# A two-layer decoder trunk: three quarters of each MLP's first matrix by Strassen's method, laced with the second matrix

## The chip, the cores and the metric

The kernel runs on one core of a Trainium2 chip. The metric is the device time of one execution in microseconds (us); lower is better. TensorE multiplies, VectorE and ScalarE work between the products, GpSimd helps outside the MLPs, SyncE (SP) issues the DMAs.

## The reference

Two layers act on a residual stream h of 528 tokens (16 meta tokens and 512 others) by 1024 features. Each layer adds a token mixer (a retention and convolution mixer in the first layer, stick-breaking attention in the second) and then an MLP. The output is h without the meta tokens, so the second layer's MLP needs only 512 tokens. What the change touches is the MLP, with w1 of 1024 x 4096 and w2 of 4096 x 1024:

```python
def sq_relu_mlp(h, w1, w2):
    return jnp.square(jax.nn.relu(h @ w1.astype(h.dtype))) @ w2.astype(h.dtype)
h = h + sq_relu_mlp(rmsnorm(h, norm_mlp_g[layer]), mlp_w1[layer], mlp_w2[layer])
```

## The kernel before

Everything is held transposed: h is eight tiles of 128 features by 528 tokens (`h[m]`), so a product has weights as the stationary operand (128 x 128) and tokens as the moving columns. Each float32 operand is used as a high and a low part, and each product is three matmuls (`products`, L280): high x high, high x low, low x high.

**Weight blocks.** A unit is a block of weights for one 128-row piece of an output: 1024 x 128 values, a 512 KB tile of 128 x 1024. `unit_order` (L94) writes down all 218 in the order of use: 40 of the first mixer's w_in, 16 of w_out, 64 of the first MLP, 24 of attention (queries, keys and values for each p of 0 to 7), 10 of its output, 64 of the second MLP. `load` (L163) has SP fetch the next block into one of two `raw` tiles. `prepare` (L176) takes it apart: ScalarE copies it to the high tile `whi` (L195), VectorE subtracts that to get `wlo` (L196); both have three buffers. `gemm` (L286) calls `weights`, which hands out the oldest prepared unit and prepares the one two places behind it; then `gemm` runs 8 x 3 products into a PSUM tile `mm` of two banks. There are two such tiles. A block is 48 matmuls over 264 columns where all 528 tokens are needed (two halves, each in a bank), and 24 matmuls over 512 columns in the second layer's MLP.

**The MLP** (`mlp`, L793) goes through `MLP_STEPS` (L116): four chunks of w1 of eight blocks each, and w2's four chunks between and behind them. After the first block `rstd` works out the normalisation factor `rb` of every token. Each w1 block's result is evicted by one VectorE operation (L808: maximum with 0, times `rb`), squared twice on ScalarE (L810, high part, and L811) and brought to a low part by VectorE (L812). Each w2 block is added to `h[m]` by VectorE (L387).

**What sets the order.** Outside the MLPs the kernel is written inside `tc.manual_schedule(engines=...)`: TensorE, VectorE, ScalarE and GpSimd then issue in the order in which the program emits their instructions, while SP's order stays the scheduler's. In the MLPs of the kernel before the scheduler orders all engines. In attention, queries, keys and values of p each start with `weights`, and so emit the load of the unit two ahead; the K copies of p (L968) are emitted by the chain that `keys` leaves behind, in the first step of the queries of p + 1, behind that unit's load.

## Time and profile before

| | us |
|---|---|
| median of 3 runs (1399.53 to 1400.27) | 1400.21 |
| the profiled execution | 1400.1 |
| its span in the profile | 1398.3 |
| TensorE busy in the span | 1377.2 |
| VectorE busy | 878.2 |
| ScalarE busy | 606.3 |
| GpSimd busy | 358.0 |

The span begins and ends with the profile's first and last instruction; the execution's own time has 1.8 us around it. The granted clock of TensorE is 0.998 of full speed over the span. Busy time of a matmul is modelled from its own start to the end of its passage, so neighbours overlap: what a matmul costs in a dense stretch is the distance between starts.

### The profile page before, as it was taken

The page shows a single profiled execution, that of the slowest core. Times are in us where ns is not written, and L with a number is a line of the kernel's source. Part 1 is how long each engine was busy: PE and PEld are TensorE (multiplying, and loading weights), DVE is VectorE, ACT ScalarE, POOL GpSimd, SP SyncE. Part 2 cuts the span into 40 slices and gives each one's busy share as a digit, 9 for nine tenths or more (in the row PEclk, how much of TensorE's full clock was granted, in tenths as well). Part 3 has the DMA queues.
Part 4 walks back from the last instruction along what each step waited for, and adds up shares of the span by engine and source line. Part 5 has one row for each costly group of instructions (what it writes and reads, how often), then busy time and mean ns, then how long its engine had stood idle before and what let it go on. Part 6 is the DMA issues. An engine that isn't in the chain of part 4 may idle for free.

```text
span 1398.3 us, 23379 instructions
## 1 busy us (share of the span) xinstructions
PE 1377.2 (98%) x9396; PEld 1270.3 (91%) x9396; DVE 878.2 (63%) x1461; ACT 606.3 (43%) x1136; POOL 358.0 (26%) x414
## 2 busy tenths in 40 slices
PE   8999999999999999999999999998999999999998
PEld 7999999999999999999999888997877888888887
DVE  5998999966344434334345899999985443434332
ACT  5434545567443313223132677776554422313220
POOL 2656455356500000000016433335640000000000
PEclk9999999999999999999999999999999999999999
DMA  5322221122322222222322534333323223232332
GB/s 189 106 91 86 66 71 67 62 76 93 100 96 92 91 91 92 91 91 91 91 91 88 141 107 122 107 107 91 91 91 101 95 93 103 91 106 91 98 105 83
DMA packets 39643, 134.00 MB, mean 96 GB/s; under 512 B 4976, under 2 KB 5104, under 8 KB 39536
## 3 DMA queue, kind: packets, MB, share of 16 engines
q1 hardware_dynamic: 39536, 132.52, 30.3%
q8 instruction: 74, 1.21, 0.4%
q14 instruction: 33, 0.27, 0.1%
HBM read 117.69 MB, written 2.10 MB: 86 GB/s over the span
## 4 chain that ended last, share of the span: by engine, by line
PE 91%; DVE 6%; issue 1%; ACT 1%; POOL 0%; DMA 0%; POOLq 0%; SPq 0%; ACTq 0%; DVEq 0%
PE mm L284 72%; PE qk L284 10%; PE pz L1034 1%; PE po L1066 1%; DVE E L1043 1%; PE pw L1056 1%; PE po L696 1%; DVE mT L1077 1%; PE po L700 1%; PE po L698 0%; DVE acc L492 0%; DVE hdn L595 0%; DMA h<-xT 0%; PE pv L682 0%; PE pt L754 0%
## 5 line engine op out<-in xcount | busy, mean ns | idle before, releaser
L195 ACT CAST whi<-raw 128x256 fp32r<-128x256 f32 (+1 forms) x338 | 212.2, 659 | 490.3 <-PE mm L284 455.2
L196 POOL TENSOR_TENSOR wlo<-raw,whi 128x256 fp32r<-128x256 f32 (+1 forms) x334 | 280.6, 859 | 284.1 <-ACT whi L195 134.6
L196 DVE TENSOR_TENSOR wlo<-raw,whi 128x1024 fp32r<-128x1024 f32 (+1 forms) x134 | 165.3, 1234 | 23.0 <-ACT whi L195 15.8
L387 DVE TENSOR_TENSOR h<-mm,h 128x528 f32<-128x528 f32 (+1 forms) x64 | 44.9, 701 | 207.7 <-PE mm L284 207.7
L492 DVE SCALAR_TENSOR_TENSOR acc<-cx,ptm,acc 128x526 f32<-128x526 f32 (+28 forms) x232 | 157.6, 740 | 3.5 <-ACT cx L487 3.5
L284 PE MATMUL mm<-xnh,whi 128*128 128x264 f32 x640 | 135.6, 294 | 0.0
L284 PE MATMUL mm<-xnl,whi 128*128 128x264 f32 x640 | 130.8, 285 | 3.1 <-DVE xnl L320 2.7
L284 PE MATMUL mm<-xnh,wlo 128*128 128x264 f32 x640 | 129.9, 285 | 0.0
L284 PE MATMUL mm<-x1h,whi 128*128 128x264 f32 x512 | 104.1, 285 | 0.0
L284 PEld LDWEIGHTS mm<-xnl,whi 128*128 128x128 f32 x640 | 100.1, 190 | 4.1 <-DVE xnl L320 3.0
L284 PEld LDWEIGHTS mm<-xnh,whi 128*128 128x128 f32 x640 | 100.9, 190 | 2.9 <-issue 1.3
L284 PE MATMUL mm<-x1l,whi 128*128 128x264 f32 x512 | 103.2, 283 | 0.0
L284 PE MATMUL mm<-x1h,wlo 128*128 128x264 f32 x512 | 102.8, 282 | 0.0
L284 PE MATMUL mm<-x3l,whi 128*128 128x512 f32 x256 | 99.7, 390 | 0.5 <-DVE x3l L320 0.5
L284 PE MATMUL mm<-x3h,whi 128*128 128x512 f32 x256 | 100.0, 391 | 0.0
L284 PE MATMUL mm<-x3h,wlo 128*128 128x512 f32 x256 | 99.6, 389 | 0.0
L284 PEld LDWEIGHTS mm<-xnh,wlo 128*128 128x128 f32 x640 | 99.6, 190 | 0.0
L334 POOL TENSOR_TENSOR n2s<-n2q,n2q 128x528 f32<-128x528 f32 x1 | 1.9, 1865 | 334.7 <-ACT n2q L353 334.7
L284 PE MATMUL qk<-x2h,whi 128*128 128x264 f32 (+1 forms) x320 | 82.9, 323 | 0.5 <-ACT kraw L926 0.5
L808 DVE SCALAR_TENSOR_TENSOR r<-mm,m0rb 128x528 f32<-128x528 f32 x32 | 22.6, 707 | 93.7 <-PE mm L284 93.7
L284 PEld LDWEIGHTS mm<-x1l,whi 128*128 128x128 f32 x512 | 79.5, 188 | 0.0
L284 PEld LDWEIGHTS mm<-x1h,whi 128*128 128x128 f32 x512 | 79.0, 188 | 0.1
(400 smaller groups left out, 3333.3 us busy)
## 6 DMA issues: line engine op xcount, KB each, us to landing
raw<-wts SPq DMA_DIRECT2D x217, 512.0 KB, 3.5
Q<-qhl SPq DMA_DIRECT2D x32, 256.0 KB, 4.5
K<-khl SPq DMA_DIRECT2D x32, 132.0 KB, 3.6
h<-xT SPq DMA_DIRECT2D x8, 264.0 KB, 6.1
out<-h SPq DMA_DIRECT2D x8, 256.0 KB, 2.0
ctm<-con SPq DMA_DIRECT2D x1, 790.0 KB, 6.9
raw<-wts SPq DMA_DIRECT2D x2, 256.0 KB, 4.0
ca<-con SPq DMA_DIRECT2D x1, 256.0 KB, 6.0
```

What stands on the lines that cost most here:

```text
L195: copy(hi[:, ks], raw[:, ks])
L196: eng.tensor_tensor(lo[:, ks], raw[:, ks], hi[:, ks].bitcast(F32), ALU.subtract)
L284: nc.tensor.matmul(p, a[:, k, :], b[:, sl], start=(first and t == 0), stop=(last and t == 2))
L387: nc.vector.tensor_tensor(v2(h[m][:, :n], n), ps, v2(h[m][:, :n], n), ALU.add)
L492: nc.vector.scalar_tensor_tensor(a, cxf[:, s:T], tap(j, s), a, ALU.mult, ALU.add)
L696: nc.tensor.matmul(po[:n, :256], st[:n, :n], vk[:n], start=True, stop=Pst is None)
L700: nc.tensor.matmul(po[:, 256:], kt[:n], vk[:n], start=True, stop=True)
L808: nc.vector.scalar_tensor_tensor(v2(r, n), ps, 0.0, v2(rb[:, :n], n), ALU.max, ALU.mult)
L1034: nc.tensor.matmul(pz[:, :w], Q2[a][:, t, q * P:(q + 1) * P], K2[a][:, k0:k0 + w], start=(t == 0), stop=(t == 1 and i > 0))
L1043: nc.vector.tensor_tensor_scan(E[:, 1:n], kp[:, :n - 1], zero.to_broadcast([P, n - 1]), 1.0, ALU.mult, ALU.add)
L1056: nc.tensor.transpose(px[:, q * P:(q + 1) * P], Ws[a, q][:, (kb - q) * P:(kb - q + 1) * P], ident)
L1066: nc.tensor.matmul(po[a][:, :KQ[kb]], vs[:, kb, a], wt[kb], start=(kb == 3 and t == 0), stop=False)
```

## The change

It takes chunks 1 to 3 of w1 in both layers by Strassen's method (in the form with seven products and fifteen additions, on 2 x 2 quarters). A pair of w1 blocks, rows m = 2i and 2i + 1, is a 2 x 2 matrix of half blocks A11, A12, A21, A22 (512 of the 1024 inputs by 128 outputs); the moving operand is quartered by inputs (features 0 to 511 and 512 to 1023) and by tokens (first and second half). Seven products of half blocks, each 12 matmuls over 264 (256) columns into one bank, take the place of eight. The sums are:

- of weights, on VectorE, for each pair: S1 = A21 + A22, S2 = S1 + A11, S3 = A11 + A21, S4 = S2 + A12 (`Pairs.sum`; the signs are put into the moving side);
- of the moving operand, once per layer: T1, T2, T3 in `differences(k)` for k = 0 to 3, written in the first chunk's rows 1, 3, 4 and 6 ahead of the row's eviction, and T4 in `difference4(k)`, which overwrites half of x during chunk 1. A T costs two scaled copies and three copies on ScalarE and seven operations on VectorE, of 264 (256) columns each;
- of results, on VectorE: seven additions from PSUM per pair, and one copy on ScalarE.

Chunk 0 stays as it was. A unit `s_` holds two products (half blocks) in the order of `PRODUCTS`; behind every second one stands a w2 block of the chunk before, and chunk 3's w2 blocks come last, as before. The products use four banks in turn, two of a tile that is idle in the MLP. The pairs' blocks come through three tiles of their own (`raw2`), loaded again as a pair's last use is emitted. From the second row of chunk 0 on, the MLP's TensorE, VectorE, ScalarE and GpSimd instructions are in written order. Scaling by `rb` and the squares are the same, the latter two products later (`later`, `tick`).

The diff, cut to its core (columns of the quarters: `hw` = n // 2):

```diff
-MLP_STEPS = [(1, 0), (1, 1), (2, 0), (1, 2), (2, 1), (1, 3), (2, 2), (2, 3)]
+NPAIR = NK // 2
+H = NK // 2
+PRODUCTS = [(kind, i) for i in range(NPAIR) for kind in ("A11", "A12", "S2", "S3", "S1", "A22", "S4")]
 def mlp_units(layer):
...
+    units = [(f"w1_{layer}", 0, m * P) for m in range(NK)]
+    for c in range(1, 4):
+        w2 = [(f"w2_{layer}", (c - 1) * D, m * P) for m in range(NK)]
+        for j in range(len(PRODUCTS) // 2):
+            units.append((f"s_{layer}", c, j))
+            if j % 2:
+                units.append(w2.pop(0))
+        units += w2
+    return units + [(f"w2_{layer}", 3 * D, m * P) for m in range(NK)]
...
-            nc.sync.dma_start(raws[u][:, ks], wts[u, :, ks])
+            nc.sync.dma_start(raws[u][:, ks], wts[place[plain[u]], :, ks])
+    pieces, pairs = [], []
+
+    class Pairs:
...
+        def load(self):
+            while self.live < 3 and self.todo:
+                c, m = self.todo.pop(0)
+                t = self.pl.tile([P, NK, P], F32, tag="raw2", name=f"pr{self.layer}{c}{m}", bufs=3)
+                nc.sync.dma_start(t, wts[place[f"w1_{self.layer}", 0, c * D + m * P]])
+                self.raw[c, m] = t
+                self.live += 1
...
+        def done(self, c, i, row):
+            self.live -= 1
+            self.load()
...
+        def start(self, c, i):
+            if ("S1", c, i) not in self.sums:
+                self.sum("S1", c, i, self.a(c, i, 1, 0), self.a(c, i, 1, 1))
+                self.sum("S2", c, i, self.a(c, i, 0, 0), self.sums["S1", c, i])
+
+        def prepare(self, hi, lo, c, j):
+            todo = PRODUCTS[2 * j:2 * j + 2]
+            for q, (kind, i) in enumerate(todo):
+                ks = slice(q * H, q * H + H)
+                if kind == "S2":
+                    self.start(c, i)
+                src = self.sums[kind, c, i] if kind[0] == "S" else self.a(c, i, int(kind[1]) - 1, int(kind[2]) - 1)
+                nc.scalar.copy(hi[:, ks], src)
+                nc.vector.tensor_tensor(lo[:, ks], src, hi[:, ks].bitcast(F32), ALU.subtract)
+                if kind == "A11" and (c, 2 * i + 1) in self.raw:
+                    self.start(c, i)
+                elif kind == "S2":
+                    self.sum("S3", c, i, self.a(c, i, 0, 0), self.a(c, i, 1, 0))
+            for kind, i in todo:
+                seen = self.used.setdefault((c, i), set())
+                seen.add(kind)
+                if "S1" in seen and "+" not in seen:
+                    self.sum("S4", c, i, self.a(c, i, 0, 1), self.sums["S2", c, i])
+                    seen.add("+")
+                if {"+", "A12"} <= seen and "0" not in seen:
+                    seen.add("0")
+                    self.done(c, i, 0)
+                if kind == "A22":
+                    self.done(c, i, 1)
...
-        if u == len(raws):
-            load()
-        raw = raws[u]
         hi = wp.tile([P, NK, P], F32R, tag="whi", name=f"whi{u}", bufs=3)
         lo = wp.tile([P, NK, P], F32R, tag="wlo", name=f"wlo{u}", bufs=3)
         name = order[u][0]
         ready.append((name, hi, lo))
+        if name[:2] == "s_":
+            pairs[-1].prepare(hi, lo, *order[u][1:])
+            return
+        if state["plain"] == len(raws):
+            load()
+        raw = raws[state["plain"]]
+        state["plain"] += 1
...
+    def mlp(layer, x, s, n, mine, banks, after):
+        hw = n // 2
+        first, second = slice(0, hw), slice(hw, n)
...
+            tsets = {t: [tuple(pl.tile([P, hw], F32R, tag=f"T{t}{e}{k}", name=f"T{layer}{t}{e}{k}") for e in "hl")
+                         for k in range(H)] for t in (1, 2, 3)}
...
+            def differences(k):
...
+                x12, x22 = temp("h", k)
+                t1, t2 = temp("l", k)
+                t3, u4 = temp("h", H + k)
+                lo_, up = h[k], h[H + k]
+                nc.scalar.activation(x12, lo_[:, second], AF.Copy, scale=g(k))
+                nc.scalar.activation(x22, up[:, second], AF.Copy, scale=g(H + k))
+                stt = nc.vector.scalar_tensor_tensor
+                stt(t1, lo_[:, first], g(k), x12, ALU.mult, ALU.subtract)
+                stt(t2, t1, -1.0, x22, ALU.mult, ALU.subtract)
+                nc.vector.tensor_tensor(t3, x22, x12, ALU.subtract)
+                stt(u4, up[:, first], g(H + k), t2, ALU.mult, ALU.add)
+                for t, src in ((1, t1), (2, t2), (3, t3)):
+                    nc.scalar.copy(tsets[t][k][0], src)
+                for t, src in ((1, t1), (2, t2), (3, t3)):
+                    hi, lo = tsets[t][k]
+                    nc.vector.tensor_tensor(lo, src, hi.bitcast(F32), ALU.subtract)
+                t4.append(u4)
+
+            def difference4(k):
+
+                hi, lo = (t[:, second] for t in x[k])
+                nc.scalar.activation(hi, t4[k], AF.Copy, scale=-1.0)
+                nc.vector.scalar_tensor_tensor(lo, t4[k], -1.0, hi.bitcast(F32), ALU.mult, ALU.subtract)
...
+            def squares(dst, r, name):
+                q = sp.tile([P, T], F32, tag="sq", name=f"q{layer}{name}")[:, :n]
+                nc.scalar.activation(dst[0][:, :n], r, AF.Square)
+                nc.scalar.activation(q, r, AF.Square)
+                return lambda: nc.vector.tensor_tensor(dst[1][:, :n], q, dst[0][:, :n].bitcast(F32), ALU.subtract)
...
+            what = f"w1_{layer}"
+            ps = gemm(what, x, n)
+            rb = rstd(s, f"m{layer}")
+            work.load()
+            manual = ExitStack()
+            for m in range(NK):
+                if m:
+                    ps = gemm(what, x, n)
+                if m in (1, 3, 4, 6):
+                    differences(len(t4))
+                r = row(f"0{m}")
+                nc.vector.scalar_tensor_tensor(v2(r, n), ps, 0.0, v2(rb[:, :n], n), ALU.max, ALU.mult)
+                squares(hidden(0, m), r, f"0{m}")()
+                if m == 0:
+                    manual.enter_context(tc.manual_schedule(engines=engines))
...
+            moving = {"A11": (x, 0, first), "A12": (x, H, first), "S4": (x, H, second), "A22": (x, 0, second),
+                      "S1": (tsets[1], 0, slice(0, hw)), "S2": (tsets[2], 0, slice(0, hw)), "S3": (tsets[3], 0, slice(0, hw))}
...
+                def finish(i, e, op):
+                    r = rows[e]
+                    stt(r, r, 0.0, rb[:, :n], op, ALU.mult)
+                    m, c_ = 2 * i + e, c
+
+                    def square():
+                        low = squares(hidden(c_, m), r, f"{c_}{m}")
+                        later(1, low)
+                    later(2, square)
+
+                def product(kind, i, w, half):
+                    src, k0, sl = moving[kind]
+                    b = state["bank"] = (state.get("bank", 0) + 1) % 4
+                    if b < 2:
+                        ps = banks[:, b, :hw]
+                    else:
+                        ps = pax.tile([P, 512], F32, tag="ax", name=f"pp{layer}{c}{i}{kind}")[:, :hw]
+                    for k in range(H):
+                        hi, lo = w[0][:, half * H + k, :], w[1][:, half * H + k, :]
+                        xh, xl = (t[:, sl] for t in src[k0 + k])
+                        for t, (l, rr) in enumerate(((hi, xh), (hi, xl), (lo, xh))):
+                            nc.tensor.matmul(ps, l, rr, start=k == 0 and t == 0, stop=k == H - 1 and t == 2)
+                    add = lambda dst, y: nc.vector.tensor_tensor(dst, ps, y, ALU.add)
+                    if kind == "A11":
+                        nc.scalar.copy(p1, ps)
+                    elif kind == "A12":
+                        rows[0] = row(f"{c}{i}0")
+                        add(rows[0][:, first], p1)
+                    elif kind == "S2":
+                        add(u2, p1)
+                    elif kind == "S3":
+                        add(u3, u2)
+                    elif kind == "S1":
+                        rows[1] = row(f"{c}{i}1")
+                        add(rows[0][:, second], u2)
+                        add(rows[1][:, second], u3)
+                    elif kind == "A22":
+                        add(rows[1][:, first], u3)
+                        finish(i, 1, ALU.min)
+                    elif kind == "S4":
+                        add(rows[0][:, second], rows[0][:, second])
+                        finish(i, 0, ALU.max)
+                    tick()
+
+                def back(m):
+                    ps = gemm(f"w2_{layer}", hid[c - 1], n, each=lambda k: tick() if k % 2 else None)
+                    nc.vector.tensor_tensor(v2(h[m][:, :n], n), ps, v2(h[m][:, :n], n), ALU.add)
+
+                for j in range(len(PRODUCTS) // 2):
+                    w = weights(f"s_{layer}")
+                    for half in range(2):
+                        product(*PRODUCTS[2 * j + half], w, half)
+                    if c == 1 and j < 2:
+                        for k in range(2 * j, 2 * j + 2):
+                            difference4(k)
+                    if j % 2:
+                        back(j // 2)
+                back(NK - 1)
+            while queue:
+                tick()
+            manual.close()
+            return after(hid[3])
...
-    s = mlp(0, setD, s, T, (actA, "A"), after0)
+    s = mlp(0, setD, s, T, (actA, "A"), cx, after0)
...
-    psum, pmm, pax, _ = psums()
+    psum, pmm, pax, pcx = psums()
+    cy = pcx.tile([P, 2, 512], F32, name="cy")
...
-    mlp(1, setF, s, SEQ, None, after1)
+    mlp(1, setF, s, SEQ, (act, "B"), cy, after1)
```

## Rows read from the trace of the kernel before

**Rows 1.** The page's first part: busy time, share, instructions of each engine.
```profile
PE 1377.2 (98%) x9396; PEld 1270.3 (91%) x9396; DVE 878.2 (63%) x1461; ACT 606.3 (43%) x1136; POOL 358.0 (26%) x414
```

**Rows 2.** The chain that ended last, in order of time: start, length, engine and line.
```profile
389.92 364.58 PE mm L284 x3024
...
1051.82 342.85 PE mm L284 x1512
```

**Rows 3.** Busy time by engine, clock and DMA in these two stretches.
```profile
389.92:754.49 364.57, 364.57 (x3025) 364.57 (x3025) 149.39 (x175) 109.56 (x141) 17.54 (x23) 1.00 0.29 91
1051.82:1394.67 342.85, 342.83 (x1512) 283.36 (x1511) 139.40 (x159) 98.78 (x127) 0.00 (x0) 1.00 0.31 98
```

**Rows 4.** Timeline of PE in attention: start, length; three more 128x256 matmuls lie between.
```profile
863.73 0.28 PE L1066 MATMUL po<-wTh,vs 128*128 128x256 f32 x1
...
864.21 0.27 PE L992 MATMUL pm<-ca,vT 128*128 128x128 f32 x1
```

**Rows 5.** Groups by form on PEld: busy us, mean ns, idle before and releasers.
```profile
L284 PEld LDWEIGHTS mm<-x1l,whi 128*128 128x128 f32 x512 | 79.5, 188 | 0.0
```

**Rows 6.** Groups by form on DVE (VectorE), the same columns.
```profile
L196 DVE TENSOR_TENSOR wlo<-raw,whi 128x1024 fp32r<-128x1024 f32 x132 | 163.9, 1242 | 22.9 <-ACT whi L195 15.8
...
L387 DVE TENSOR_TENSOR h<-mm,h 128x528 f32<-128x528 f32 x40 | 28.3, 707 | 129.1 <-PE mm L284 129.1
...
L1045 DVE TENSOR_TENSOR sp<-sp,E 128x512 f32<-128x512 f32 x16 | 10.6, 660 | 0.0
...
L977 DVE TENSOR_TENSOR vT<-qk,n2rb 128x264 f32<-128x264 f32 x16 | 6.1, 419 | 0.0
...
L812 DVE TENSOR_TENSOR hid00l<-q,hid00h 128x528 fp32r<-128x528 f32 x8 | 5.6, 701 | 0.3 <-ACT q L811 0.3
...
L196 DVE TENSOR_TENSOR wlo<-raw,whi 128x512 fp32r<-128x512 f32 x2 | 1.4, 694 | 0.1
```

**Rows 7.** Timeline of DVE at the start of both MLPs.
```profile
394.39 0.71 DVE L808 SCALAR_TENSOR_TENSOR r<-mm,m0rb 128x528 f32<-128x528 f32 x1
...
396.60 1.22 DVE L196 TENSOR_TENSOR wlo<-raw,whi 128x1024 fp32r<-128x1024 f32 x1
397.74 0.70 DVE L812 TENSOR_TENSOR hid00l<-q,hid00h 128x528 fp32r<-128x528 f32 x1
...
1056.27 0.69 DVE L808 SCALAR_TENSOR_TENSOR r<-mm,m1rb 128x512 f32<-128x512 f32 x1
```

**Rows 8.** Timeline of ACT (ScalarE): the two squares of one row, then the next row's.
```profile
396.47 0.64 ACT L810 ACTIVATE hid00h<-r 128x528 fp32r<-128x528 f32 x1
397.01 0.63 ACT L811 ACTIVATE q<-r 128x528 f32<-128x528 f32 x1
397.55 0.63 ACT L810 ACTIVATE hid00h<-r 128x528 fp32r<-128x528 f32 x1
```

**Rows 9.** Groups by form on ACT.
```profile
L195 ACT CAST whi<-raw 128x1024 fp32r<-128x1024 f32 x134 | 140.9, 1052 | 481.5 <-PE mm L284 448.8 <-issue 31.6 <-DMA raw<-wts 1.2
...
L1057 ACT CAST wTh<-pw 128x512 fp32r<-128x512 f32 x16 | 9.4, 586 | 6.2 <-PE pw L1056 5.8
```

**Rows 10.** Timeline of SP's queue in attention.
```profile
769.26 8.05 SPq L168 DMA_DIRECT2D raw<-wts  x2
777.36 2.39 SPq L968 DMA_DIRECT2D K<-khl  x4
```

**Rows 11.** Line 168 up to 777.2 us: count, duration, first and last start.
```profile
L168 SPq DMA_DIRECT2D raw<-wts x128: 327/328/1134, 1.6 to 777.0; - x128
```

**Rows 12.** Line 168 over the whole span: from issue to landing.
```profile
DMA to landing us min/median/max: 3.1/3.5/6.5
```

More of the change, by code (lines that the diff above doesn't have):

```diff
@@ L156, in trunk @@
     h = [act.tile([P, T], F32, name=f"h{m}") for m in range(NK)]
-    state = {"unit": 0}
+    state = {"unit": 0, "plain": 0}
     order = unit_order()
+    place = {b: i for i, b in enumerate(blocks())}
+    plain = [b for b in order if b in place]
     raws, ready = [], []
@@ L167, in load, with __init__, a, sum @@
             ks = slice(i * NK // n, (i + 1) * NK // n)
-            nc.sync.dma_start(raws[u][:, ks], wts[u, :, ks])
-    pieces = []
+            nc.sync.dma_start(raws[u][:, ks], wts[place[plain[u]], :, ks])
+    pieces, pairs = [], []
+    class Pairs:
+        def __init__(self, layer, pl):
+            self.layer, self.pl = layer, pl
+            self.todo = [(c, m) for c in range(1, 4) for m in range(NK)]
+            self.raw, self.sums, self.used = {}, {}, {}
+            self.live = 0
+        def load(self):
[5 more added lines that the diff above has]
+                self.live += 1
+        def a(self, c, i, row, half):
+            return self.raw[c, 2 * i + row][:, half * H:half * H + H]
+        def done(self, c, i, row):
+            self.live -= 1
+            self.load()
+        def sum(self, name, c, i, x, y):
+            t = self.pl.tile([P, H, P], F32, tag="S", name=f"{name}_{self.layer}{c}{i}", bufs=3)
+            nc.vector.tensor_tensor(t, x, y, ALU.add)
+            self.sums[name, c, i] = t
+        def start(self, c, i):
[26 more added lines that the diff above has]
+                    self.done(c, i, 1)
@@ L1186, in layout @@
         mats[f"w2_{layer}"] = a(mlp_w2)[layer]
-    order = unit_order()
+    order = blocks()
     wts = np.empty((len(order), P, NK, P), np.float32)
```

70 lines of the change are left out of this document (38 added, 32 removed).

## The prediction

> **What bounds the kernel now.** I read the page's busy shares first: TensorE is busy for 1377.2 of 1398.3 us, VectorE for 878.2 [rows 1]. The chain of waits says whether that share is a bound: in time order it holds two unbroken pieces, 3024 matmuls in 364.58 us and 1512 matmuls in 342.85 us [rows 2]. They are the first and the second layer's MLP: 63 blocks of 48 matmuls over 264 columns, and 63 of 24 over 512. The busy table of these stretches closes it: TensorE has no gap, VectorE works 149.39 and 139.40 us, ScalarE 109.56 and 98.78, the DMA engines are at 0.29 to 0.31, the granted clock is 1.00 [rows 3]. So in both MLPs a matmul costs its spacing: 364.58 / 3024 = 0.1206 us at 264 columns (a block 5.79), 342.85 / 1512 = 0.2268 at 512 (a block 5.44).
>
> **TensorE: what goes, what comes.** Per layer, 24 blocks of w1 become 84 half-block products of 12 matmuls. First layer: 24 x 48 = 1152 matmuls become 1008, both over 264 columns: 144 x 0.1206 = 17.4 us less. Second layer: 576 x 0.2268 = 130.6 us become 1008 matmuls over 256 columns. The nearest row is in attention: four matmuls over 256 columns into one bank, each with its own weights, take 864.21 - 863.73 = 0.48 us [rows 4], 0.12 each to the 0.01 us of the view; a line through 264 and 512 columns gives 0.1206 - 8 x 0.000428 = 0.117. I take 0.1175: 118.4 us, 12.2 less. Bounds: 0.1206 (nothing gained from 8 fewer columns) leaves 9.1; half of 0.2268 gains 16.3. Together **29.6 us** (26.5 to 33.7). More product starts cost nothing: 63 starts lie inside each unbroken piece.
>
> This needs weight loads to stay hidden, one per matmul. A load takes 0.188 us in the record, longer than the 0.1206 spacing [rows 5], so loads overlap the matmuls. [...]
>
> **VectorE and ScalarE in the laced part.** A pair of rows takes TensorE 84 matmuls and on average 1.75 w2 blocks: 10.1 + 10.1 = 20.3 us (9.9 + 9.5 = 19.4 in the second layer). VectorE's work for it, from the forms [rows 6]: seven low halves of 512 columns (0.69), four sums (0.66), seven additions of 264 columns from PSUM (0.42), two scalings (0.71), two low parts of squares (0.70), 1.75 times a whole block's low part (1.24) and w2's addition (0.71). Independent neighbours start before the last one ends: 397.74 follows 396.60 by 1.14 us where one takes 1.22 to 1.24 [rows 6, 7], so I count each 0.07 short, and one that reads its neighbour's result 0.03 long. Sum: 4.3 + 2.5 + 2.5 + 1.5 + 1.3 + 3.2 = 15.3 us, 75% (79% in the second layer; before: 41%). ScalarE's work (seven copies of 0.59, four squares of 0.64, 1.75 copies of 1.05 [rows 8, 9]: 8.5 us) is under half. Each block is prepared two units ahead, at least two half blocks (5.8 us) before use; the longest half-block preparation (copy 0.6, low part, sum, copy, low part) is about 3.4 us, so in steady state it is covered and I cost it at nothing. If VectorE falls behind by more than the cover, the next w2 block is what comes late, since only two half blocks stand ahead of it.
>
> **The start of each layer's MLP is not covered.** There all engines now follow the written order, and the differences stand ahead of the eviction of rows 1, 3, 4 and 6. After an eviction's end E, ScalarE's two squares end at E + 1.19 [rows 8]; then come its copy of the next block (1.05 [rows 9], from E + 1.08), VectorE's low part (1.24, to E + 3.40) and the next eviction (to E + 4.05). The differences' seven operations of 264 columns (0.42 each, 0.35 apart, one dependence 0.1 more) add 2.55: E + 6.60. Two PSUM tiles alternate, so matmul block m + 2 waits for eviction m. First layer: E0 = 395.10 [rows 7], E1 = 401.7, but block 2 ends at 401.3: block 3 is 0.57 late (with 0.16 for the restart). E2 = 405.8, E3 = 412.4, E4 = 419.0, E5 = 423.0 hold nobody. Row 6 has a half block with two sums as well: E6 = 430.7. Block 7 ends at 430.8, the first half block at 433.7. The second's last weights come at E6 + 4.5 = 435.2 (0.25 late); E7 = 435.9, so w2's first block has weights at 439.3 where TensorE is free at 436.8: 2.6 late. Sum 3.4 us. Second layer, the same from E0 = 1056.96 [rows 7] with blocks of 5.44: 1.05 + 0.6 + 0.85 + 2.6 = 5.1. Together **8.5 us**. Bounds: 0 if copies and squares slip in between; 17.5 if no VectorE instruction overlaps its neighbour, dependent starts are 0.03 apart and each handoff is 0.1.
>
> VectorE's instructions overlap their neighbours by 0.07 us and more [rows 7]. [...] Spacing every instruction by its full duration, my walk gives 13.6 us of start stalls in place of 8.5. By the rule the result would be 1384; I give that 0.1 within the forecast's own chance, since the rows side against it.
>
> **DMA and SP's queue.** Bytes are the same: 24 of 32 w1 blocks come through the pair tiles. A new transfer could hold up w2's: both are issued by SP, and a pair's load waits for its tile. SP isn't bound to the written order, and the rows show the order it gets. The second of the two transfers that precede the K copies at 777.36 is the 128th of weights [rows 10, 11]; the first block came in two, so it is block 127: 40 + 16 + 64 blocks before attention, then the seventh there, the queries of p = 2. The program writes this load at the start of the keys of p = 1, behind those K copies (p = 0, written during the queries of p = 1). So loads are moved ahead as soon as their buffer allows. Then w2's load, whose buffer is long free, should pass the pair's; landing takes 3.5 us, at most 6.5 [rows 12], and I cost it at nothing. With 6.5 everywhere the pair tiles' landing adds 2.6.
>
> **Sum.** 1400.1 us (this execution; span 1398.3; median of the runs 1400.21) - 29.6 + 8.5 = **1379.0 us**. About 0.2%, 2.8 us, is what a measurement of this kernel can tell from no change.
>
> **Rivals.**
> 1. *w2's load waits behind the pairs' in SP's queue; slower.* In written order, four of a chunk's eight w2 loads stand right behind pair loads (after half-block units 2, 5 to 6, 9, 12 to 13, of 0 to 13). A pair tile is free when VectorE ends its last sum, about when the next two half blocks start. From there: transfer 3.5, copy 1.05, low part 1.24, handoffs 0.2 = 6.0 us; the cover is 5.8 (5.6) us, and VectorE runs 1 to 2 us behind TensorE, which makes 1.2 to 2.4 us a block (3.0 more at the longest landing of rows 12). I price it at 2.1; 24 of them are 50 us: 1379 + 50 = **1429 us**. It decides from (29.6 - 8.5) / 24 = 0.9 us per block. Against it: rows 10 and 11, and transfers at 0.3 of capacity.
> 2. *VectorE paces the laced part.* If handoffs lengthen its work by a fifth, start stalls and the first w2 blocks lose 22.6 us in the same walk: **1393 us**; at three tenths every chunk loses and the walk has 51.3 us of stalls, 1422. For: 75% on one in-order engine that ScalarE feeds. Against: overlapping neighbours.
> 3. *Weight loads show at 256 columns.* At one load's 0.188 per matmul the second layer loses 59 us: about 1450. Rows 4 exclude it.
> 4. *The start costs nothing*: 1370.
>
> **How the numbers follow.** Forecast 0.62 (own range 1370 to 1388); rival 2 short of losing the gain 0.14; no visible change 0.06; rival 1 with all else that makes it slower 0.14 (rival 3 in it, 0.01); rival 4 or better 0.04. The range of 8 in 10, 1369 to 1400, holds the forecast (start 0 to 17.5, TensorE 26.5 to 33.7), rival 2 and half of the two small cases: 0.62 + 0.14 + 0.05. Faster: 0.62 + 0.14 + 0.04 = 0.80; same 0.06; slower 0.14.
>
> **What would show it.** Right: matmul counts 144 lower in the first MLP and 432 higher in the second; spacing 0.1206 over 264 columns and 0.117 to 0.118 over 256; TensorE's gaps only in the first 50 us of each MLP, at the third plain block and at w2's first block, ended by VectorE; VectorE about three quarters busy after that; SP's w2 loads ahead of pair loads. Wrong: gaps in front of w2 blocks through all chunks, with ScalarE's copy waiting for a DMA (rival 1) or VectorE without idle time (rival 2); a spacing above 0.121 over 256 columns (rival 3).

## The result, and the profile after

The changed kernel takes 1381.99 us, median of 4 runs (1380.88 to 1383.26); the kernel before took 1399.87 beside it (4 runs, 1398.18 to 1400.27). The ratio is 0.9875, with a 95% interval of 0.9858 to 0.9892: faster by 1.1 to 1.4%. The profiled execution took 1382.29 us (span 1380.5), 17.8 us less than the one of before (1400.1).

The first thing to do with two such profiles is to cut both at the same places: the matmuls that sum the squares of the first MLP's norm (n1ps), the first query matmul of attention (qk), the sums of the second MLP's norm (n3ps), the last matmul. The timeline of PE, kernel after (start, length, operation, idle before and releaser); the rows between the cuts are TensorE's gaps and, at 1079.82 and 1080.66, two products:

```profile
387.19 1.05 PE L435 MATMUL n1ps<-n1s,ca 128*128 128x264 f32 x4
...
394.69 0.36 PE L372 MATMUL mm<-x1h,whi 128*128 128x264 f32 x1 [0.64 <-DVE r L949]
...
434.48 0.39 PE L996 MATMUL cx<-T03h,whi 128*128 128x264 f32 x1 [0.44 <-ACT snap L999]
...
448.01 0.36 PE L996 MATMUL cx<-x1h,whi 128*128 128x264 f32 x1 [1.57 <-DVE r L997]
...
741.09 0.39 PE L372 MATMUL qk<-x2h,whi 128*128 128x512 f32 x1
...
1037.80 1.12 PE L435 MATMUL n3ps<-n3s,ca 128*128 128x512 f32 x2 [0.40 <-POOL n3s L422]
...
1045.18 0.47 PE L372 MATMUL mm<-x3h,whi 128*128 128x512 f32 x1 [0.78 <-DVE r L949]
...
1079.82 0.28 PE L996 MATMUL pp110A<-x3l,whi 128*128 128x256 f32 x1
...
1080.66 0.28 PE L996 MATMUL pp110A<-x3h,wlo 128*128 128x256 f32 x1
...
1084.13 0.39 PE L996 MATMUL cy<-T13h,whi 128*128 128x256 f32 x1 [1.75 <-ACT snap L999]
...
1376.45 0.39 PE L372 MATMUL mm<-hid13h,wlo 128*128 128x512 f32 x1
```

The same cuts in every profile of this study (us, between the starts of these matmuls; the kernels are described below):

| kernel | to the first MLP | first MLP | attention | second MLP |
|---|---|---|---|---|
| before | 388.87 | 365.46 | 296.36 | 343.57 |
| after | 387.20 | 353.89 | 296.71 | 338.66 |
| e1_rows | 386.89 | 355.21 | 297.06 | 342.23 |
| e2_spq | 387.75 | 388.30 | 296.49 | 374.64 |
| e3_place | 388.71 | 352.00 | 296.55 | 336.90 |
| e4_plain256 | 387.09 | 365.46 | 296.32 | 353.43 |
| e5_low1 | 389.39 | 354.98 | 296.69 | 341.68 |
| e7_start | 387.77 | 350.77 | 296.79 | 335.75 |
| e8_both | 387.00 | 350.79 | 296.79 | 334.00 |
| e9_banks | 389.12 | 354.01 | 297.12 | 337.81 |
| e10_low2 | 386.77 | 359.43 | 296.42 | 350.23 |
| e11_order | 387.36 | 350.14 | 296.55 | 334.00 |

The first MLP gained 11.57 us, the second 4.91. The 1.67 us of the first column are not the change's: no kernel here alters that stage, and it lies between 386.77 and 389.39 in all of them. That is also why an MLP, read from one profile, tells apart what whole times can't: before and e4 share the first MLP's code and have 365.46 both, e7 and e8 350.77 and 350.79, while the stage ahead spreads over 2.6 us and attention over 0.8. It doesn't where a transfer decides: after, e3 and e9 share the first MLP's code too, and have 353.89, 352.00 and 354.01, with and without one gap that is read below.

The page's busy line, which answers to [rows 1]: 288 more matmuls (-144 and +432), 22.3 us less of TensorE, 189.5 us more of VectorE.

```profile
PE 1354.9 (98%) x9684; PEld 1267.7 (92%) x9684; DVE 1067.7 (77%) x1909; ACT 677.8 (49%) x1328; POOL 357.4 (26%) x414
```

The chain that ended last (start, length) is no longer two pieces as in [rows 2]. The rows to read are the one DMA in it since the kernel's first load, and w2's blocks of 24 matmuls in the second layer: 5.55 us in chunk 1, 5.47 in chunk 2, ten at 5.47 at the end, where each took 342.85 / 63 = 5.44 before.

```profile
437.67 6.31 DMA pr<-wts
...
1085.84 5.55 PE mm L372 x24
...
1170.44 5.47 PE mm L372 x24
...
1322.18 54.68 PE mm L372 x240
```

Busy time by engine (the columns of [rows 3]): the two MLPs, then the laced parts behind their last gap. There TensorE has none, and VectorE works 173.57 of 235.06 us and 180.57 of 236.51, 74 and 76%.

```profile
387.89:741.09 353.20, 350.55 (x2883) 349.94 (x2881) 245.29 (x399) 145.38 (x238) 17.37 (x23) 1.00 0.29 89
1038.36:1376.45 338.09, 335.56 (x1945) 296.37 (x1944) 234.47 (x384) 135.45 (x223) 0.00 (x0) 1.00 0.30 95
448.01:683.07 235.06, 235.06 (x1934) 235.06 (x1935) 173.57 (x284) 93.65 (x151) 0.00 (x0) 1.00 0.30 93
1085.67:1322.18 236.51, 236.51 (x1491) 214.25 (x1490) 180.57 (x301) 97.17 (x159) 0.00 (x0) 1.00 0.32 99
```

So the difference between gained and forecast has two sources, which can be summed from the distances between the starts of neighbouring matmuls. The first is **five gaps**: 0.92, 0.72 and 1.86 us between starts in the first layer, 1.16 and 2.03 in the second; with the slower restarts, and less the spacing, 3.4 and 3.0 us. The second is a **wider spacing**. In the first layer plain and w2's matmuls stand 0.1211 us apart, products 0.1220, against 0.1206 before; in the second layer products stand 0.1194 (in the two-bank tile, called cx in the first layer and cy in the second) or 0.1200 apart (in the one-bank tiles pp: 7 steps in 0.84 us above), w2's matmuls on average 0.2289 against 0.2267. That is 2.4 and 4.3 us more than the prediction's terms. The experiments ask where both come from.

One gap needs its queue to be read. The product that starts at 1084.13 waited for ScalarE's copy of the first product out of PSUM (snap, L999). ScalarE and VectorE, timelines, kernel after:

```profile
1081.73 0.63 ACT L934 ACTIVATE hid10h<-r 128x512 fp32r<-128x512 f32 x1 [1.36 <-DVE r L949]
...
1082.79 1.03 ACT L283 CAST whi<-raw 128x1024 fp32r<-128x1024 f32 x1
1083.72 0.36 ACT L999 COPY snap<-cy 128x256 f32<-128x256 f32 x1
```

```profile
1075.92 0.69 DVE L949 SCALAR_TENSOR_TENSOR r<-mm,m1rb 128x512 f32<-128x512 f32 x1
...
1081.01 0.68 DVE L949 SCALAR_TENSOR_TENSOR r<-mm,m1rb 128x512 f32<-128x512 f32 x1
```

The copy stands behind row 7's two squares and w2's weight copy in ScalarE's queue; the squares wait for row 7's eviction at 1081.01, some 3 us after row 7's last matmul, because the differences of row 6 and its half block had put VectorE behind. And the product that waits writes the *other* bank of the two-bank tile cy.

The first layer's gap of 1.86 us, at the eighth product, has the same shape. VectorE, timeline, kernel after:

```profile
444.01 0.69 DVE L223 TENSOR_TENSOR S<-pr 128x512 f32<-128x512 f32 x1 [3.00 <-DMA pr<-wts]
...
447.44 0.42 DVE L997 TENSOR_TENSOR r<-cx,snapu 128x264 f32<-128x264 f32 x1
```

A pair's load landed 6.31 us after its issue; VectorE stood 3.00 us for it, and behind the sum that needed it came the additions. The last of them out of cx ended at 447.86, the product started at 448.01. By the order of banks in `product`, the addition read the fifth product out of bank 1, and the eighth product writes bank 0.

### The profile page after: what moved, and what is told of

Same layout as the page of the kernel before. It is cut to its first block, busy times and chain, and to the rows that moved or that the text cites. A ratio compares the mean times of both kernels' runs of the same rounds, so it can differ in the third digit from the quotient of the medians.

```text
span 1380.5 us, 24559 instructions
## 1 busy us (share of the span) xinstructions
PE 1354.9 (98%) x9684; PEld 1267.7 (92%) x9684; DVE 1067.7 (77%) x1909; ACT 677.8 (49%) x1328; POOL 357.4 (26%) x414
## 4 chain that ended last, share of the span: by engine, by line
PE 87%; DVE 8%; ACT 2%; issue 1%; DMA 1%; POOL 0%; SPq 0%; ACTq 0%; DVEq 0%; POOLq 0%
PE mm L372 51%; PE qk L372 11%; PE cy L996 4%; PE cx L996 4%; PE pz L1253 2%; PE po L1285 1%; PE pw L1275 1%; PE po L784 1%; DVE wlo L284 1%; DVE x3l L408 1%; DVE mT L1296 1%; ACT whi L283 1%; PE po L788 1%; DVE E L1262 1%; PE po L786 1%
## 5 line engine op out<-in xcount | busy, mean ns | idle before, releaser
L283 ACT CAST whi<-raw 128x256 fp32r<-128x256 f32 (+1 forms) x290 | 161.4, 593 | 205.0 <-PE mm L372 123.0
L284 DVE TENSOR_TENSOR wlo<-raw,whi 128x1024 fp32r<-128x1024 f32 (+1 forms) x86 | 106.3, 1237 | 19.3 <-ACT whi L283 18.4
L239 DVE TENSOR_TENSOR wlo<-S,whi 128x512 fp32r<-128x512 f32 x96 | 65.1, 689 | 31.2 <-ACT whi L238 29.8
L238 ACT CAST whi<-S 128x512 fp32r<-128x512 f32 x96 | 57.9, 615 | 54.2 <-DVE S L223 24.4
L372 PE MATMUL qk<-x2h,wlo 128*128 128x264 f32 (+1 forms) x320 | 77.0, 306 | 0.0
L372 PE MATMUL qk<-x2l,whi 128*128 128x264 f32 (+1 forms) x320 | 76.9, 305 | 0.0
L1262 DVE TENSOR_TENSOR_SCAN E<-kp,oz 128x527 f32<-128x527 f32 (+1 forms) x64 | 61.1, 975 | 1.5 <-ACT kp L1258 1.5
L372 PEld LDWEIGHTS qk<-x2h,whi 128*128 128x128 f32 x320 | 53.4, 191 | 2.6 <-ACT kraw L1145 0.9
L372 PEld LDWEIGHTS qk<-x2h,wlo 128*128 128x128 f32 x320 | 51.5, 188 | 2.7
L372 PEld LDWEIGHTS qk<-x2l,whi 128*128 128x128 f32 x320 | 51.8, 188 | 1.1
```

Source lines behind the costliest of these rows:

```text
L238: nc.scalar.copy(hi[:, ks], src)
L239: nc.vector.tensor_tensor(lo[:, ks], src, hi[:, ks].bitcast(F32), ALU.subtract)
L283: copy(hi[:, ks], raw[:, ks])
L284: eng.tensor_tensor(lo[:, ks], raw[:, ks], hi[:, ks].bitcast(F32), ALU.subtract)
L372: nc.tensor.matmul(p, a[:, k, :], b[:, sl], start=(first and t == 0), stop=(last and t == 2))
L1262: nc.vector.tensor_tensor_scan(E[:, 1:n], kp[:, :n - 1], zero.to_broadcast([P, n - 1]), 1.0, ALU.mult, ALU.add)
```

## The experiments

**e1_rows: the differences behind the squares, on other rows.**

```
-                if m in (1, 3, 4, 6):
-                    differences(len(t4))
                 r = row(f"0{m}")
                 nc.vector.scalar_tensor_tensor(v2(r, n), ps, 0.0, v2(rb[:, :n], n), ALU.max, ALU.mult)
                 squares(hidden(0, m), r, f"0{m}")()
+                if m in (2, 3, 4, 5):
+                    differences(len(t4))
```

> The changed kernel with the four sets of differences after the eviction and the squares of rows 2 to 5, in place of ahead of the eviction of rows 1, 3, 4 and 6. Theory (the start's stalls come from VectorE's backlog: the first differences delay rows 0 and 1, those of row 6 delay row 7's eviction, and behind it in ScalarE's queue stands the first product's copy out of PSUM): all five stalls of the changed kernel go, 0.92 + 0.72 + 1.86 us in the first layer and 1.16 + 2.03 in the second, less the 0.12 to 0.23 that a matmul takes anyway: 5.9 us less, about 1376.1. Rival 1 (the last of the first layer's stalls, 1.86, is the landing of a pair's load and has nothing to do with the differences): only the other four go, 4.2 us less, 1377.8. Rival 2 (the start's work is only moved, and VectorE's backlog meets w2's first block): new gaps of 2 to 3 us at w2's first block in each layer, no gain.

Measured: 1386.22 us (ratio to before 0.9908, 0.9893 to 0.9923), 4.2 us slower than the changed kernel where 5.9 less was expected: a miss. The first gap of both layers is gone and the eighth product's is 0.58 us, but the fourth product's has grown to 2.73 and 3.78 us. VectorE's timeline shows why:

```profile
1064.26 0.68 DVE L947 SCALAR_TENSOR_TENSOR r<-mm,m1rb 128x512 f32<-128x512 f32 x1
1066.16 0.69 DVE L936 TENSOR_TENSOR hid10l<-q,hid10h 128x512 fp32r<-128x512 f32 x1 [1.22 <-ACT q L935]
...
1070.68 0.68 DVE L947 SCALAR_TENSOR_TENSOR r<-mm,m1rb 128x512 f32<-128x512 f32 x1
```

A row with differences takes VectorE 6.42 us (1064.26 to 1070.68), 1.22 of it waiting for the squares, and a row takes TensorE 5.44. Spread over rows 1, 3, 4 and 6, as the change had them, the backlog is partly worked off in between; on four rows in a row it only grows. The theory of the backlog stands; my cure fed it. The table of stretches adds a second price (the third number from the end of a row is the granted clock):

```profile
1083.00:1086.60 3.60, 0.10 (x1) 0.00 (x0) 2.14 (x4) 2.40 (x5) 0.00 (x0) 0.82 0.00 0
1086.60:1089.00 2.40, 2.39 (x11) 2.40 (x12) 2.40 (x5) 2.23 (x6) 0.00 (x0) 0.50 0.29 27
1089.00:1092.00 3.00, 3.00 (x10) 2.42 (x10) 2.90 (x8) 1.14 (x2) 0.00 (x0) 0.50 0.63 213
```

After the gap the clock is at 0.50, and matmuls over 512 columns stand 0.43 us apart in place of 0.23.

**e7_start: the differences in three parts, on rows 1 to 4.**

```
                 nc.scalar.activation(x22, up[:, second], AF.Copy, scale=g(H + k))
+                yield
...
                 stt(u4, up[:, first], g(H + k), t2, ALU.mult, ALU.add)
+                yield
...
+                part = differences(len(t4)) if m in (1, 2, 3, 4) else iter("abc")
+                next(part)
                 r = row(f"0{m}")
                 nc.vector.scalar_tensor_tensor(v2(r, n), ps, 0.0, v2(rb[:, :n], n), ALU.max, ALU.mult)
-                squares(hidden(0, m), r, f"0{m}")()
+                low = squares(hidden(0, m), r, f"0{m}")
+                next(part)
+                low()
+                next(part)
```

> The changed kernel with the differences on rows 1 to 4 (no row has a half block to prepare as well) and split in three: ScalarE's two scalings stand ahead of a row's eviction, VectorE's four operations between the eviction and the squares' low part, where it waited 1.2 us for ScalarE, the copies and low parts after it. VectorE then needs about 5.0 us a row with differences, in place of 6.4 to 6.7, and a row takes TensorE 5.44 to 5.79. Theory (backlog of VectorE's serial chain is the only cause of the start's stalls, the late copy of the first product included): no gap at the third plain block and none at the fourth product, 1.6 less 0.35 us in the first layer and 3.2 less 0.5 in the second: 4.0 us less than the changed kernel, about 1378. The gap of 1.86 us in the first layer, at the eighth product, is a pair's load that landed late and may come or not. Rival (the fourth product waits for the first's copy because w2's weight copy stands ahead of it on ScalarE, whatever VectorE does): the gaps of 0.7 and 2.0 us stay, 2 us less at most.

Measured: 1376.69 us (0.9835, 0.9822 to 0.9849), 5.3 less than the changed kernel where 4.0 was expected. A gap of 0.38 us remains at the first layer's third block, none in the second. VectorE's timeline, one row:

```profile
1047.55 0.69 DVE L952 SCALAR_TENSOR_TENSOR r<-mm,m1rb 128x512 f32<-128x512 f32 x1
1048.16 0.47 DVE L913 SCALAR_TENSOR_TENSOR t1l<-h,pt,t1h 128x256 f32<-128x256 f32 x1
...
1049.81 0.69 DVE L939 TENSOR_TENSOR hid10l<-q,hid10h 128x512 fp32r<-128x512 f32 x1
...
1052.99 0.69 DVE L952 SCALAR_TENSOR_TENSOR r<-mm,m1rb 128x512 f32<-128x512 f32 x1 [0.35 <-PE mm L372]
```

The same work fits into the row (1047.55 to 1052.99 is 5.44 us), and now VectorE waits for TensorE at its end. The MLPs are 3.1 and 2.9 us shorter than the changed kernel's. In the second layer this is what the start cost. In the first the difference holds the gap at the eighth product as well. e3 has the changed kernel's code there, lacks that gap and takes 352.00 us; against it e7 gains 1.2.

**e9_banks: the two-bank tile made two tiles (second layer).**

```
-    cy = pcx.tile([P, 2, 512], F32, name="cy")
+    cy = [pcx.tile([P, 512], F32, name=f"cy{i}") for i in range(2)]
```

> The changed kernel with the second layer's two-bank PSUM tile for products made two tiles of one bank each. In the changed kernel the fourth product waited 2.03 us for ScalarE's copy of the first, out of the other bank of the same tile. Theory (the wait belongs to the tile, not to the bank): the fourth product starts without a gap; the next late thing is w2's first block, whose weights were ready at 1085.08 where TensorE would then be free at 1083.6: a gap of about 1.4 us there, 0.5 us less in all. Rival (the fourth product waits for its own weights): the gap of 2.0 us stays where it is.

Measured: 1383.9 us in one run; the second MLP is 0.85 us shorter. The timeline of PE:

```profile
1084.58 0.28 PE L996 MATMUL pp110S<-T12h,wlo 128*128 128x256 f32 x1
1084.70 0.28 PE L996 MATMUL cy<-T13h,whi 128*128 128x256 f32 x1
...
1087.62 0.50 PE L372 MATMUL mm<-hid10h,wlo 128*128 128x512 f32 x1 [0.54 <-DVE wlo L284]
```

The fourth product starts 0.12 behind its neighbour, without a gap: the wait belonged to the tile, not to the bank. What is late next is the low part of w2's first block, by about 1 us in several steps (1.4 was expected). So the prediction's 2.6 us at that block was there, smaller, and hidden behind a wait that I had not seen.

**e2_spq: SP bound to the written order.**

```
-                    manual.enter_context(tc.manual_schedule(engines=engines))
+                    manual.enter_context(tc.manual_schedule(engines=engines | {nc.sync.engine}))
```

> The changed kernel with SP bound to the written order in both MLPs, so that two of w2's loads that now pass the pairs' loads stand behind them. By the prediction's rival 1: half of w2's blocks wait 2.1 us, 24 of them, about 50 us more, 1432, with gaps ahead of w2's blocks in all chunks. If the transfers are back sooner than the walk assumed (the pair's tile is free well before the next but one half block ends): gaps of less than 0.9 us a block, 0 to 10 us more.

Measured: 1453.44 us (1.0388, 1.0367 to 1.0409), 71 us slower than the changed kernel. SP's queue, ScalarE, VectorE, PE, and the table of stretches around one of the waits:

```profile
455.37 0.33 SPq L210 DMA_DIRECT2D pr<-wts  x1
455.74 0.43 SPq L194 DMA_DIRECT2D raw<-wts  x1
```

```profile
460.37 1.04 ACT L283 CAST whi<-raw 128x1024 fp32r<-128x1024 f32 x1 [6.48 <-DMA raw<-wts]
```

```profile
461.44 1.23 DVE L284 TENSOR_TENSOR wlo<-raw,whi 128x1024 fp32r<-128x1024 f32 x1 [4.92 <-ACT whi L283]
462.59 0.42 DVE L997 TENSOR_TENSOR r<-cx,snap 128x264 f32<-128x264 f32 x1
```

```profile
463.16 0.56 PE L996 MATMUL cx<-T01h,whi 128*128 128x264 f32 x1 [3.48 <-DVE r L997]
```

```profile
459.50:463.10 3.60, 0.17 (x2) 0.00 (x0) 1.66 (x3) 2.08 (x3) 0.00 (x0) 0.93 0.04 15
463.10:465.70 2.60, 2.54 (x11) 2.57 (x12) 1.79 (x4) 0.00 (x0) 0.00 (x0) 0.50 0.32 41
```

w2's load goes out right behind the pair's, ScalarE's copy waits for it until 460.37, VectorE's low part for the copy, and in VectorE's queue behind that stand the additions that empty the products' tile: TensorE stands still at a *product*, 3.5 us, one step ahead of the block whose weights are late. Summed over the distances between starts, the gaps are about 49 us longer than in the changed kernel, and the matmuls at 0.22 and 0.43 us behind them cost about 21 us more. That rival 1 had 50 us for the waiting is in part luck: it had 24 waits of 2.1 us in front of w2's blocks, and e2 has 20 of 0.7 to 5.1 us in both MLPs (the changed kernel 3), all in front of products; the clock came on top.

All 20 of these products write bank 0 of the two-bank tile, and the last read of that tile before each was of bank 1. In the rows above, w2's low part is there at 462.67, and without the wait for the tile the product would have been over at about 461.0 (459.39, its neighbour's start, and 13 spacings): an estimate of 1.7 us in place of 3.5. No run splits the tile and binds SP, so how much of the 71 us is the order's alone stays open.

In the changed kernel itself SP is free to send w2's loads ahead, as [rows 10, 11] made me expect, and none of the waits for w2's loads is there. Eight loads of w1's plain and w2's blocks have gone out there by 435.77, ahead of the pairs'; in e2 the eighth is the one at 455.74:

```profile
380.43 55.34 SPq L194 DMA_DIRECT2D raw<-wts  x8
437.67 0.93 SPq L210 DMA_DIRECT2D pr<-wts  x2
```

**e5_low1 and e10_low2: more work for VectorE.** e5 takes the low part of one of two half blocks twice, on the changed kernel; e10 that of both, on the kernel of e8 (below), which has no gaps at the start.

```
-                nc.vector.tensor_tensor(lo[:, ks], src, hi[:, ks].bitcast(F32), ALU.subtract)
+                for _ in range(2 if q in (0,) else 1):
+                    nc.vector.tensor_tensor(lo[:, ks], src, hi[:, ks].bitcast(F32), ALU.subtract)
```

> The changed kernel with the low part of the first half block of every pair of half blocks taken twice (the same result): 3.5 more operations of 0.69 us per pair of rows, each 0.61 behind its neighbour, 2.1 us on 15.3, 14 percent more work for VectorE in the laced part, 17.5 of 20.3 us. By the prediction's second rival (a fifth more work loses the cover at w2's first blocks: 14 us) about 10 us more, 1392. If the cover of two half blocks holds: 0 to 2 us more, 1382 to 1384, and VectorE at 86 percent.

> The kernel with both edits, with the low part of both half blocks taken twice (the same result): 7 more operations of 0.69 us per pair of rows, 0.61 apart, 4.3 us on 15.3, 28 percent, 19.6 of the 20.3 us that TensorE takes for a pair in the first layer and of 19.4 in the second. With 14 percent the laced part had no gap behind the first pair. If VectorE can be filled to the end: no gaps in the first layer's laced part, and in the second 0.2 us a pair, 12 pairs, 2 to 3 us, with gaps at the start, 1378 to 1382. By the prediction's second rival (at three tenths every chunk loses): gaps in front of w2's blocks in all six chunks, over 40 us, above 1415.

Measured: e5 1387.38 us, 5.4 more than the changed kernel, between its two expectations; 1.1 and 3.0 of it in the MLPs. The fourth product's gap grew from 0.72 and 2.03 to 2.17 and 3.49 us, with a low clock behind it (0.53 on average from 438.00 to 440.50); the one of 1.86 at the eighth was not there. Behind that there is no gap in either layer, with VectorE at 209.67 of 249.00 us in the first, 84% (first row). e10: 1399.60 us, 24.9 more than e8, the whole gain of the change; VectorE at 222.00 of 242.85 us, 91% (second row), and gaps of 0.35 to 2.1 us between starts in every laced chunk, nearly all in front of products whose tile VectorE has not emptied (the waits of PE in e10: in total, times, longest).

```profile
441.00:690.00 249.00, 249.00 (x2049) 249.00 (x2048) 209.67 (x341) 100.59 (x161) 0.00 (x0) 1.00 0.30 95
```

```profile
446.85:689.70 242.85, 239.35 (x1947) 237.25 (x1948) 222.00 (x362) 94.24 (x152) 0.00 (x0) 1.00 0.28 90
```

```profile
PE cy L1016 <- DVE r L1017: 6.4, 7, 1.8
...
PE cx L1016 <- DVE r L1017: 4.7, 7, 1.4
```

So the laced part has room for 14% more on VectorE and not for 28%, with this tile: in e10 every laced gap of more than 0.5 us stands in front of a product into bank 0 of cx or cy and behind a read of bank 1, and none in front of the one-bank tiles pp. What 28% would cost with a tile for each bank was not tried. Both expectations of e10 missed: it doesn't fill to the end, and it doesn't lose 40.

**e4_plain256: 256 columns by themselves.** In the kernel before (and the views that evict the block follow):

```
+        if what == "w1_1":
+            width = n // 2
         halves = [(slice(i * width, i * width + width), ps[:, i, :width]) for i in range(n // width)]
```

> The kernel before, with the second layer's w1 blocks run as two halves of 256 columns into two banks in place of one of 512: 768 matmuls of the second layer become 1536, nothing else. It measures the spacing over 256 columns apart from Strassen's products and from VectorE's load. By the prediction's line through 264 and 512 columns: 0.1175 us, 1536 x 0.1175 - 768 x 0.2268 = 6.3 us more. If 256 columns have their own price, as the changed kernel's rows say: 0.1194 to 0.1200, 9.2 to 10.1 us more. If VectorE's load had widened it there: 0.1175 here.

Measured: 1408.15 us in one run, the second MLP 9.86 us longer. The timeline of PE: 6 matmuls in 0.72 us.

```profile
1054.86 0.40 PE L284 MATMUL mm<-x3h,whi 128*128 128x256 f32 x2
...
1055.58 0.40 PE L284 MATMUL mm<-x3h,whi 128*128 128x256 f32 x2
```

0.120 is the price of 256 columns in a kernel with neither Strassen's products nor VectorE's load.

**e3_place: the second layer's hidden tiles one behind the other.** Line 1368 passes None in place of (act, "B"), and chunks 0 and 2 get tiles of their own; the difference sets and the weight sums go into B's slots.

```
-                p_, tag = mine if c % 2 == 0 else (pl, "C")
+                p_, tag = (mine or (pl, "D")) if c % 2 == 0 else (pl, "C")
```

> The changed kernel with the second layer's chunk 0 and 2 hidden tiles in tiles of 2048 bytes one behind the other in place of slots of 2112 bytes; in exchange the sets of the differences and the weight sums move into those slots. Theory (the spacing of matmuls depends on where the moving tiles stand): w2's blocks of chunks 1 and 3 take 5.44 to 5.47 us in place of 5.55, 16 blocks, 1.3 to 1.8 us less; products over the difference sets, now in slots of 2112 bytes, leave the 0.1194 to 0.1200 that they share with all other products. Rival (TensorE's spacing widens because VectorE is busier there): 5.55 stays, since VectorE's work is the same; 0.

Measured: 1381.04 us (0.9874, 0.9857 to 0.9891), whole times that can't be told from the changed kernel's; the second MLP is 1.76 us shorter. The chain has w2's blocks of chunk 1 (first row) at 5.48, and the ten at the end at 5.44 each:

```profile
1085.31 5.48 PE mm L377 x24
...
1320.14 54.44 PE mm L377 x240
```

The products over the difference sets, now in slots of 2112 bytes, went from 0.1193 to 0.1200 us down to 0.1183 to 0.1193. VectorE's work was the same, so this part of the spacing goes by the places of the moving tiles. e5 says the same from the other side. Its laced matmuls, with VectorE at 84% (its row above) and, in the second layer, at 86% (the row below), took 249.00 / 2049 = 0.1215 and 236.00 / 1488 = 0.1586 us each, over all widths; the changed kernel's, at 74 and 76%, took 235.06 / 1934 = 0.1215 and 236.51 / 1491 = 0.1586.

```profile
1094.00:1330.00 236.00, 236.00 (x1488) 213.78 (x1487) 203.51 (x336) 97.45 (x159) 0.00 (x0) 1.00 0.30 97
```

What e3 leaves, 5.47 to 5.48 in the laced blocks of chunks 1 to 3 against 5.44 at the end, is not the places', for chunks 1 and 3 share their tiles: it stands in the first five matmuls of a block behind a product, 0.229 to 0.235 apart, where the later ones are at 0.227.

**e8_both and e11_order: versions that beat both kernels.** e8 is e7 and e3 together; e11 gives chunks 1 and 3 their places in reading order as well.

```
             t4 = []
+            for k in range(NK):
+                for e in "hl":
+                    pl.tile([P, n], F32R, tag=f"C{e}{k}", name=f"c{layer}{e}{k}")
```

> The two edits together: the differences on rows 1 to 4 in three parts, and the second layer's hidden tiles one behind the other in place of slots of 2112 bytes. If the two are independent: 4.0 + 1.8 us less than the changed kernel, about 1376. If the start's work meets the same wait elsewhere: 1380.

> The kernel with both edits (differences on rows 1 to 4 in three parts, the second layer's hidden tiles one behind the other) with one more: the hidden tiles of chunks 1 and 3 are given their places in the order in which TensorE reads them, high and low of row 0, of row 1 and so on; in the changed kernel the order of first use had scattered them. Theory (spacing depends on the places of successive moving tiles): the first layer's w2 blocks of chunk 2 and of the end, 5.84 and 5.83 us, take 5.79 to 5.80, 16 blocks, 0.6 us less, about 1374.1. Rival (the scatter does nothing, the busier VectorE does): 5.83 stays, 1374.7.

Measured: e8 1374.73 us (0.9823, 0.9809 to 0.9836), the two edits add up as expected (1.3 us beyond it). e11 1376.02 (1373.87 to 1376.23; 0.9832, 0.9818 to 0.9845): not told apart from e8 by its times; its first MLP is 0.65 us shorter, and its w2 blocks of chunk 2 and of the end, 5.84 and 5.82 us in e8, are at 5.80 and 5.79 on average (the end, ten blocks):

```profile
679.79 57.86 PE mm L377 x480
```

## Why the prediction was right, and which terms were off

The forecast was 1379.0, the profiled execution took 1382.3. From one to the other: +2.4 and +4.3 us of spacing, -2.1 us of start, -1.3 us outside the MLPs. The mechanism was right: fewer columns, hidden weight loads, VectorE and DMA covered in the laced part, a price at the start. That the sum came within 3.3 us is in part luck, since the start's error and the stages that no kernel alters took back half of the spacing's.

- **TensorE, 29.6 us.** The counts are as predicted; dense TensorE time fell by 15.0 and 7.9 us (the MLPs' gains with the gaps added back), 22.9 in all and below the stated bound of 26.5. The terms that were too good are "both over 264 columns: 144 x 0.1206" and "I take 0.1175". For 256 columns, [rows 4] had said 0.12; I replaced a row by a line through two other widths, and e4 shows that the row was right: 1008 x 0.0022 = 2.2 us. The rest, some 2.0 us in the second layer and 2.4 in the first, is a term that I didn't have: matmuls whose spacing was to stay as it was stand further apart in the changed kernel. The places of the tiles are shown for 1.3 us of w2's matmuls in the second layer (e3) and for 0.65 in the first (e11). What remains is open. For the products over 264 columns it isn't the place of the tile alone: x's own tiles, which nobody moved, are read at 0.1207 in the plain blocks and at 0.1215 (into cx) and 0.1223 (into pp) in the products.
- **Weight loads.** They stay hidden at 0.120, and rival 3 is out: in the second layer's products a load takes 0.191 (into cy) and 0.192 us (into pp) on average in the record, and the matmuls stand 0.1194 and 0.1200 apart, so loads overlap matmuls there as in [rows 5].
- **VectorE, 75 and 79%.** 74 and 76%. The cover holds with 14% more (e5) and gives way at 28% (e10), so rival 2 was a real limit at a distance. Its walk put the loss at w2's blocks; it falls on products, whose two-bank tile is emptied late, and at 28% it is 24.9 us, less than the 43 (1422 - 1379) that the walk had at 30.
- **The start, 8.5 us.** 6.4 in the profiled execution; without the eighth product's gap, which comes and goes, 4.6. That 8.5 lies near is luck, for hardly a term stands where the walk had it:
  - *A plain block.* The walk had block 3 wait for row 1's eviction, 0.57 and 1.05. Found were 0.8 and 0.9 one block earlier: the first differences stand in VectorE's queue ahead of the scaling factor `rb` and so delay row 0's eviction. The walk's further 0.6 in the second layer was not found.
  - *The second half-block unit.* 0.25 and 0.85 predicted, 0.6 and 1.9 found, by another wait: the first product's copy behind row 7's squares, and a tile of two banks that waits as one.
  - *w2's first block.* 2.6 in each layer predicted, none found, since TensorE had been held before; e9 uncovers 1 us of it.
  - *A late pair load.* The first layer's 1.86 at the eighth product. The prediction had seen landings of up to 6.5 us and put them at nothing; this one took 6.31. e3 and e9 share the first layer's code; one has no such gap, the other 1.98.
- **Overlap of VectorE's instructions.** The walk with them gave 8.5, the one that spaces every instruction by its full duration, the prediction's rule for 1384, 13.6. The 6.4 decides little between them, as its gaps are others than the walk's; the overlap itself is in the rows (in e2's above, 462.59 follows 461.44 by 1.15 where that one takes 1.23).
- **SP's queue, nothing.** Right, and e2 shows what that rested on: with this tile of two banks, the written order costs 71 us. The chance of 0.14 for that side was not idle.

## What to carry to other kernels

A row of the trace for the very shape goes before a line through other shapes. Work put on an in-order engine should go where it already waits for another engine (e7), not where its data are ready (e1): with the same operations e1 is 9.5 us slower than e7. A PSUM tile of two banks was waited for as one (e9: with two tiles in its place the gap of 2.03 us is gone), and every long wait of e2 and e10 was for the neighbour bank of such a tile: a tile for each bank is the first thing to try. Where a queue's order is the scheduler's, look at it before binding it: one word here cost four times the gain of the change.

## What the runs showed that I had not expected

**The clock.** After the changed kernel's gaps of 0.72 to 2.03 us between starts, the matmuls from the second on stood at their usual spacing, 0.12 us over 264 and 256 columns and 0.23 over 512, and the granted clock was 1.00 over the 3.4 to 4.0 us behind each. After those of 2.12 (e10), 2.17 and 3.49 (e5), 2.73 and 3.78 (e1) and 3.77 (e2) the granted clock was at 0.50 in place of 1.00, at once or within 2 us, for some microseconds (e1 from 1086.60 to 1092.00 and e2 from 463.10 to 465.70, in the rows above). The length of the gap alone does not decide: behind e2's gaps of 2.19 and 2.77 us, at 1299.74 and 1368.64, it stayed at 1.00. A wait then costs more than its length: in e2, about 21 us on 49. In the MLPs the rows at 0.50 each stand behind a gap, and each is back at 1.00 while TensorE works on (e1: 0.98 on average from 1092.00 to 1095.00, with TensorE busy for all 3.00 us). What decides between the two values is not shown.

**Places.** In w2's last blocks matmuls over 512 columns stand 0.2268 us apart (54.44 / 240, e3). In the laced blocks they stand 0.228 apart when their tiles of 2048 bytes follow one another (5.48 / 24, e3) and 0.231 in slots of 2112 bytes (5.55 / 24). Over 256 columns the slots are a little better (0.1183 to 0.1193). VectorE's load changed nothing: at 84 and 86% (e5) a laced matmul took 0.1215 us in the first layer and 0.1586 in the second, and the same at the changed kernel's 74 and 76%. What the places change I can only measure, not explain.
